# Weight sums of the first four FFN tiles: formed beside the last head's scan instead of in the FFN

## The chip, the cores and the metric

One core of a Trainium2 chip runs one layer of a diffusion backbone in float32. The metric is device time in microseconds, the median of several runs. The engines are TensorE (PE; PEld is its weight load), VectorE (DVE), ScalarE (ACT), GpSimd (POOL) and SyncE (SP), whose queue issues nearly all DMA transfers, in order.

## The reference, cut to what matters

```python
yx, _, _ = token_mixers(hx, rows, s_f, s_b, *mix_params)   # delta-rule heads | pooling, then @ w_out
x = x + gt1 * rms_norm(yx, g_post_mix)
hx = rms_norm(x, g_pre_ffn) * (1 + sc2) + sh2
x = x + gt2 * rms_norm(conv_glu_ffn(hx, w_up, conv_ffn, w_down), g_post_ffn)

def conv_glu_ffn(h, w_up, conv_w, w_down):
    gate, up = jnp.split(h @ w_up, 2, axis=-1)
    return (jax.nn.silu(depthwise_conv(gate, conv_w)) * up) @ w_down
```

There are 1024 tokens, a width of 1024, four delta-rule heads of 128, four pooling groups, and an FFN width of 2816 = 22 tiles of 128. The change touches `h @ w_up` alone: how its weights reach the matrix products.

## The kernel before, in words

**Precision.** Every float32 product is done as three products of split operands: ScalarE casts an operand to a short-mantissa high part (`split_steps`, line 259), VectorE subtracts it to get the low part. So each operand costs one ScalarE cast (`wqh`) and one VectorE subtraction (`wql`).

**Order of the work.** The kernel is a set of generators ("streams"). While the program is built, a planner (`Streams`, with the cost model `Clock`) repeatedly picks the ready stream of the lowest priority number and lets it emit its next instructions; a stream waits by yielding an event name (`signal` fires it), a count of slots (`free` returns them) or tiles that its next step reads. The outcome is a fixed instruction order on every engine and on SP's DMA queue.

**Stages around the change.** `stream_Q` (line 1098) scans the heads one after another; for head h it fires `T{h}` when it has taken three working slots, loads q, ktok and vr, forms the attention products (`dn_attn`) and then does eight scan steps (`dn_scan`, line 908), each of which goes from TensorE to VectorE (`X`), TensorE, ScalarE (`ws`, `wv`), TensorE and VectorE (`S`). Beside it `stream_G` (line 1269) runs the matrix products of the input projection as filler, with weights loaded by `stream_load`, and `pool_post` (line 1157) runs the pooling branch on VectorE. Working tiles of 128x1024 come from 13 slots (`slot`, line 282; NK = 4 and NBIG = 9). Then come the output projection in eight token tiles (`mix_load`, `stream_W`), with each tile's norm, residual and transposes (`residual`, line 1410), and the FFN.

**The up-projection.** Pairs of 512x512 blocks are multiplied by a seven-product scheme: `PROD` names, for product p = 1 to 7, its weight-side operand (block or sum of blocks of `w_up`) and its activation-side operand. Per FFN tile f the weights come as four blocks of 128x512, q11, q12, q21 and q22; four GpSimd sums form the operands of products 5, 7, 6 and 3, and products 1, 2 and 4 use q11, q12 and q22 as they are. `prep(f)` (line 1481) takes four of the eight `st` slots (NST = 8), loads the four blocks, and forms the sums in place as soon as the plain blocks have been split; since q22 is overwritten, it is loaded again for product 4 into the single buffer `st2`. Tile 2 is special: its first two operands come early as fillers and are loaded a second time into a tile `a2` of the pool `fT`. `stream_split` (line 1537) splits the operands in the order `SEQ` (line 1465) into four pairs of `wq` buffers (NWQ = 4), and `stream_up` (line 1594) does the 12 matmuls of each entry. SEQ has products 1 and 2 of tiles 0, 1 and 2 first, then the others of tiles 0 and 1, then tiles 2 to 21 interleaved by pairs. All `prep` streams start when `stream_wt` (line 1340) opens the FFN's memory at the start of the output projection. `stream_T` (line 1548) forms the activation-side sums (`T2`, `T3`, ...) and splits them.

Of the kernel before, what the change touches and what calls it, by code (L numbers as in the profile page):

```python
# [17 lines left out]
P = 128  # L18
# [7 lines left out]
NF = 22  # L26
# [101 lines left out]
class Streams:  # L128
# [10 lines left out]
    def signal(self, name):  # L139
        self.events[name] = max(self.now, self.clock.end)  # L140
# [42 lines left out]
def kernel(ctx: ExitStack, tc: tile.TileContext, I, out):  # L183
# [1156 lines left out]
    def stream_wt():  # L1340
        nonlocal wt, h2p, fa
        for e in ("Q3", "O30", "O31", "F30", "F31", "WO0", "WO1"):
            yield e
        dctx.close()
        pctx.close()
        h2p = fctx.enter_context(tc.tile_pool(name="h2", bufs=1, side="left", reuse_waits="tile"))
        for n in ("11", "21"):
            W["B" + n] = [hblock(h2p, "ha", f"b{n}{x}") for x in "hl"]
        W["hf"] = h2p.tile([P, KT, T], F32, name="hf")
        fa = fctx.enter_context(tc.tile_pool(name="ffna", bufs=1, side="left", reuse_waits="tile"))  # L1350
        wt = wctx.enter_context(tc.tile_pool(name="wtmp", bufs=2, side="left", reuse_waits="tile"))
        W["gg1"] = wt.tile([P, D], F32, name="gg1", bufs=1)
        dma(out=W["gg1"], in_=ggd[0].rearrange("k p -> (k p)").partition_broadcast(P))
        signal("WT")
        for f in range(NF):
            spawn(prep(f), 9)
        spawn(stream_split(), 8)
        spawn(stream_T(), 2)
        spawn(stream_up(), 8)
        for n, t in enumerate(ORDER):  # L1360
            if n > 1:
                yield f"H{ORDER[n - 2]}"
            W["x", t] = wt.tile([P, D], F32, name="xr")
            dma(out=W["x", t], in_=xsrc[t])
# [107 lines left out]
    CH = [f // 2 + NJ * (f % 2) for f in range(NF)]  # L1472
    A, wq, up, bank = {}, {}, {}, {}
    gd = dram.tile([NF, P, T], F32, name="gd")
    sd = dram.tile([NJ, P, 4, 512], F32, name="sd")
    td = dram.tile([NJ, P, 4, 512], F32, name="td")

    def st(name):
        return fa.tile([P, 4, P], F32, name=name, tag="st", bufs=NST)

    def prep(f):

        if f:
            yield f"pre{f - 1}"
        if f == 2:
            yield "FT"
            w = fT.tile([P, 4, 512], F32, name="a2", tag="ht", bufs=10)
            for n in range(2):
                A[f, n + 1] = w[:, n].rearrange("p (k n) -> p k n", n=P)
                dma(out=A[f, n + 1], in_=I["w_up_t"][CH[f]][:, 4 * n:4 * n + 4])  # L1490
            signal("a2")
            yield (w,)
            signal("A21")
            signal("A22")
        yield "st", 4
        src = {"11": I["w_up_t"][CH[f]][:, 0:4], "12": I["w_up_t"][CH[f]][:, 4:8],
               "21": I["w_up_t"][NF + CH[f]][:, 0:4], "22": I["w_up_t"][NF + CH[f]][:, 4:8]}
        q = {}
        for n in ("11", "21", "22", "12"):
            q[n] = st("a" + n)  # L1500
            dma(out=q[n], in_=src[n])
        signal(f"pre{f}")
        if f != 2:
            A[f, 1], A[f, 2] = q["11"], q["12"]
        yield (q["11"],)
        if f != 2:
            signal(f"A{f}1")
        yield (q["21"], q["22"])
        G.tensor_tensor(q["22"], q["21"], q["22"], ALU.add)
        A[f, 5] = q["22"]  # L1510
        yield
        G.tensor_tensor(q["21"], q["11"], q["21"], ALU.subtract)
        A[f, 7] = q["21"]
        yield f"w{f}1"
        G.tensor_tensor(q["11"], q["22"], q["11"], ALU.subtract)
        A[f, 6] = q["11"]
        yield
        signal(f"A{f}6")
        signal(f"A{f}7")
        signal(f"A{f}5")  # L1520
        yield (q["12"],)
        if f != 2:
            signal(f"A{f}2")
        yield f"w{f}2"
        G.tensor_tensor(q["12"], q["12"], q["11"], ALU.subtract)
        A[f, 3] = q["12"]
        yield
        signal(f"A{f}3")
        yield f"w{f}6"
        free("st", 1)  # L1530
        yield "st2", 1
        A[f, 4] = fa.tile([P, 4, P], F32, name="st2")
        dma(out=A[f, 4], in_=src["22"])
        yield (A[f, 4],)
        signal(f"A{f}4")

    def stream_split():
        for f, p in SEQ:
            yield "wq", 1
            yield f"A{f}{p}"  # L1540
            hi, lo = [fa.tile([P, 4, P], F32R, name=f"wq{x}", tag=f"wq{x}", bufs=NWQ) for x in "hl"]
            yield from split_steps(hi, lo, A[f, p])
            wq[f, p] = hi, lo
            signal(f"w{f}{p}")
            if p in (7, 5, 4, 3):
                free("st2" if p == 4 else "st", 1)

    def stream_T():

        nonlocal fT, fb  # L1550
        yield f"Y{ORDER[-1]}"
        hctx.close()
        fT = fctx.enter_context(tc.tile_pool(name="ffnt", bufs=1, side="right", reuse_waits="tile"))
        signal("FT")
        hf = W["hf"]
        ks = (slice(0, 2), slice(2, 4))
        b11, b12 = [hf[:, 0:4, h] for h in half]
        b21, b22 = [hf[:, 4:8, h] for h in half]
        for t in (1, 0, 2, 3):
            yield f"H{t}"  # L1560
            yield f"H{t + 4}"
            ts = slice(t * P, t * P + P)
            for x, y, z in ((b11, b12, b11), (b12, b22, b12)):
                (V if t == 3 and x is b11 else G).tensor_tensor(x[:, :, ts], y[:, :, ts], z[:, :, ts], ALU.subtract)
            yield
        wctx.close()
        yield "a2"
        fb = fctx.enter_context(tc.tile_pool(name="ffnb", bufs=1, side="left", reuse_waits="tile"))
        signal("FB")
        t2 = fT.tile([P, 4, 512], F32, name="t2f", tag="ht", bufs=10)  # L1570

        def parts(n, x, k):
            if n not in W:
                W[n] = [hblock(fT, "ht", f"{n}{y}") for y in "hl"]
            yield from split_steps(W[n][0][:, k], W[n][1][:, k], x[:, k])
            signal(f"{n}{k.start // 2}")

        for k in ks:
            V.tensor_tensor(t2[:, k], b22[:, k], b11[:, k], ALU.subtract)
        for k in ks:  # L1580
            yield from parts("T2", t2, k)
        for k in ks:
            yield from parts("T3", b12, k)
        for k in ks:
            V.tensor_tensor(b21[:, k], b21[:, k], t2[:, k], ALU.subtract)
        yield
        for n, x in (("T1", b11), ("T4", b21), ("B22", b22)):
            for k in ks:
                yield from parts(n, x, k)
        signal("TD")  # L1590
# [274 lines left out]
    spawn(stream_G(), 9)  # L1865
    spawn(stream_wt(), 2)
    spawn(stream_W(), 7)
    free("st", NST)
    free("st2", 1)
    free("wq", NWQ)  # L1870
# [77 lines left out]
```

## Time and profile before

| | us |
|---|---|
| median of three runs | 1364.37 |
| lowest, highest run | 1360.97, 1365.2 |
| the profiled execution, its own time | 1366.2 |
| its span, first to last instruction | 1364.5 |

The rows of the trace come from the profiled execution, with times in us from the span's start. A line of a timeline has start, duration, engine, line, operation, out<-in with shapes, and in brackets the idle time of the engine before it with what ended that. All instructions are recorded by one helper, line 123, so tiles tell them apart. Matmuls are pipelined, so their durations overlap.

### The profile page before, as it was taken

The numbers are of one execution on the slowest core, as the hardware profiler recorded it, in microseconds if no ns is written. First come the engines' busy times: TensorE is split into PE (matmuls) and PEld (weight loads), VectorE is DVE, ScalarE is ACT, GpSimd is POOL, SyncE is SP. The second block draws the span as 40 slices with busy tenths as digits, with TensorE's granted clock in tenths as the row PEclk, the third lists the DMA queues.
The fourth block names the chain that finished last, engine by engine and source line by source line (L and its number), as shares of the span: only waits on it lengthen the run. The fifth ranks groups of instructions, "written<-read, shape, count | busy, mean of one in ns | idle before, by whom it ended". The sixth has DMA issues, their size and how long they took to land.

```text
span 1364.5 us, 23950 instructions
## 1 busy us (share of the span) xinstructions
PE 1276.8 (94%) x8655; PEld 1006.3 (74%) x8655; DVE 1008.1 (74%) x2027; ACT 624.9 (46%) x1478; POOL 338.3 (25%) x431
## 2 busy tenths in 40 slices
PE   5878999998999799987988999999999999999997
PEld 1447668776878678856776788888888887888885
DVE  1876655656778788449879999999877778755674
ACT  3545956355676435344544333323323335644540
POOL 0562334141141510003012333333332320000122
PEclk8989989998999899988998999999999999999999
DMA  9513655545462323384322566666334339976661
GB/s 335 204 40 99 199 175 142 167 123 173 143 185 78 73 86 96 116 263 152 124 86 83 198 247 220 238 234 227 141 116 139 118 138 294 302 230 192 191 211 62
DMA packets 145302, 226.55 MB, mean 166 GB/s; under 512 B 53440, under 2 KB 66592, under 8 KB 142368
## 3 DMA queue, kind: packets, MB, share of 16 engines
q1 hardware_dynamic: 144752, 224.61, 49.9%
q8 instruction: 68, 1.11, 0.3%
q14 instruction: 50, 0.41, 0.1%
q10 hardware_dynamic: 432, 0.42, 0.1%
HBM read 164.77 MB, written 60.21 MB: 165 GB/s over the span
## 4 chain that ended last, share of the span: by engine, by line
PE 72%; DVE 13%; DMA 6%; ACT 3%; issue 3%; POOL 2%; SPq 0%; DVEq 0%; ACTq 0%; POOLq 0%
PE pa L123 27%; PE pc L123 23%; PE pb L123 22%; DVE hf L123 2%; DMA w_m<-in_wmod 1%; DMA w_mod<-in_wmod 1%; DVE x L123 1%; DVE gtmp L123 1%; POOL sX L123 1%; DVE rs_a L123 1%; POOL stmp L123 1%; DVE wql L123 1%; DVE yrs L123 1%; DMA wo_st<-in_w_out 1%; DMA sc<-blk_x 1%
## 5 line engine op out<-in xcount | busy, mean ns | idle before, releaser
L123 POOL TENSOR_TENSOR a<-a,a 128x512 f32<-128x512 f32 x88 | 143.4, 1630 | 320.4 <-DVE wql L123 158.5
L123 ACT CAST wqh<-a 128x512 fp32r<-128x512 f32 x132 | 80.9, 621 | 168.6 <-PE pb L123 76.8
L123 DVE TENSOR_TENSOR op<-dst,op 128x512 fp32r<-128x512 f32 x154 | 104.0, 715 | 58.6 <-ACT op L123 58.0
L123 PE MATMUL pa<-h_hi,w_hi 128*128 128x512 f32 x320 | 138.9, 434 | 2.5 <-ACT jk L123 1.2
L123 ACT CAST op<-dst 128x512 fp32r<-128x512 f32 x154 | 90.2, 620 | 98.6 <-PE pc L123 35.7
L123 PE MATMUL pa<-h_hi,w_lo 128*128 128x512 f32 x320 | 129.4, 404 | 1.6 <-DVE w_lo L123 1.6
L123 PE MATMUL pa<-h_lo,w_hi 128*128 128x512 f32 x320 | 130.4, 407 | 0.0
L123 PE MATMUL pc<-op 128*128 128x512 f32 x528 | 121.7, 391 | 0.0
L123 DVE TENSOR_TENSOR wql<-a,wqh 128x512 fp32r<-128x512 f32 x132 | 104.6, 795 | 17.2 <-ACT wqh L123 17.1
L123 PEld LDWEIGHTS pc<-op 128*128 128x128 f32 x528 | 99.0, 188 | 21.9 <-DVE graw L123 0.4
L123 DVE TENSOR_TENSOR hf<-hf 128x512 f32<-128x512 f32 (+1 forms) x109 | 92.3, 853 | 7.1 <-ACT hf L123 6.7
L123 POOL TENSOR_TENSOR hf<-hf,gg 128x512 f32<-128x512 f32 x16 | 21.2, 1350 | 214.2 <-ACT t L123 214.2
L123 PEld LDWEIGHTS pa<-h_hi,w_hi 128*128 128x128 f32 x320 | 61.2, 191 | 16.0 <-issue 3.0
L123 DVE SCALAR_TENSOR_TENSOR hf<-graw,sm,hf 128x1024 f32<-128x1024 f32 x44 | 71.3, 1621 | 0.7
L123 PEld LDWEIGHTS pa<-h_hi,w_lo 128*128 128x128 f32 x320 | 60.9, 190 | 14.1 <-DVE w_lo L123 1.8
L123 DVE SCALAR_TENSOR_TENSOR cv<-raw,sm,cv 128x1024 f32<-128x1024 f32 x48 | 62.6, 1305 | 11.4 <-ACT cv L123 10.8
L123 PEld LDWEIGHTS pa<-h_lo,w_hi 128*128 128x128 f32 x320 | 61.5, 192 | 9.4 <-issue 2.0
L123 PE MATMUL pa<-op 128*128 128x512 f32 x198 | 50.6, 391 | 0.0
L123 PE MATMUL pb<-op 128*128 128x512 f32 x198 | 50.4, 390 | 0.0
L123 ACT ACTIVATE hf<-hf 128x1024 f32<-128x1024 f32 x22 | 23.4, 1062 | 58.0 <-DVE hf L123 58.0
L123 ACT ACTIVATE ws<-pc,btg 128x128 f32<-128x128 f32 x80 | 27.0, 367 | 48.4 <-PE pc L123 48.0
L123 DVE TENSOR_TENSOR w_lo<-w_st,w_hi 128x512 fp32r<-128x512 f32 x40 | 27.6, 693 | 26.8 <-ACT w_hi L123 16.5
(385 smaller groups left out, 3356.4 us busy)
## 6 DMA issues: line engine op xcount, KB each, us to landing
a<-in_w_up_t SPq DMA_DIRECT2D x90, 256.0 KB, 3.2
w_m<-in_wmod SPq DMA_DIRECT2D x64, 256.0 KB, 3.3
hf<-in_w_down SPq DMA_DIRECT2D x22, 512.0 KB, 4.2
td<-hf SPq DMA_DIRECT2D x11, 1024.0 KB, 4.8
gd<-hf SPq DMA_DIRECT2D x22, 512.0 KB, 2.6
sd<-hf SPq DMA_DIRECT2D x11, 1024.0 KB, 5.4
dst<-sd SPq DMA_DIRECT2D x44, 256.0 KB, 4.5
dst<-td SPq DMA_DIRECT2D x44, 256.0 KB, 4.4
```

Source lines behind the costliest of these rows:

```text
L123: return f(*a, **k)
```

## The change

A new stream `sums_first`, with priority 6, starts at the event `T3`. For each of the tiles 0 to 3 it takes two working slots, loads the 128x1024 weights of both halves (512 KB each), forms the same four sums in place on GpSimd, and stores both to a new DRAM tensor `ad`. When all are done it fires `pre`. `prep_first` takes the place of `prep(0)` to `prep(3)`: it loads the 28 operands of these tiles one by one in the order of SEQ, each into one `st` slot, plain blocks from `w_up` and sums from `ad`. `stream_split` returns one slot for each entry of these tiles. The reload through `st2` and the tile `a2` go for tiles 0 to 3; from tile 4 on `prep` is as before, after the last of the 28 loads. Of the last four SEQ entries of tile 3, three lie behind the first entry of tile 4.

```diff
@@ -1352,7 +1352,8 @@
         W["gg1"] = wt.tile([P, D], F32, name="gg1", bufs=1)
         dma(out=W["gg1"], in_=ggd[0].rearrange("k p -> (k p)").partition_broadcast(P))
         signal("WT")
-        for f in range(NF):
+        spawn(prep_first(), 9)
+        for f in range(NPRE, NF):
             spawn(prep(f), 9)
         spawn(stream_split(), 8)
         spawn(stream_T(), 2)
@@ -1472,26 +1473,56 @@
     CH = [f // 2 + NJ * (f % 2) for f in range(NF)]
     A, wq, up, bank = {}, {}, {}, {}
     gd = dram.tile([NF, P, T], F32, name="gd")
+    NPRE = 4
+    ad = dram.tile([NPRE, 2, P, T], F32, name="ad")
     sd = dram.tile([NJ, P, 4, 512], F32, name="sd")
     td = dram.tile([NJ, P, 4, 512], F32, name="td")
 
     def st(name):
         return fa.tile([P, 4, P], F32, name=name, tag="st", bufs=NST)
 
+    def sums_first():
+
+        yield "T3"
+        for f in range(NPRE):
+            yield "s", 2
+            x = [slot("pre") for _ in range(2)]
+            for n in range(2):
+                dma(out=x[n], in_=I["w_up_t"][n * NF + CH[f]].rearrange("p k n -> p (k n)"))
+            yield tuple(x)
+            (q11, q12), (q21, q22) = [[y[:, h] for h in half] for y in x]
+            for o, y, z, op in ((q22, q21, q22, ALU.add), (q21, q11, q21, ALU.subtract), (q11, q22, q11, ALU.subtract),
+                                (q12, q12, q11, ALU.subtract)):
+                G.tensor_tensor(o, y, z, op)
+                yield
+            for n in range(2):
+                dma(out=ad[f, n], in_=x[n])
+            free_slots(*x)
+        signal("pre")
+
+    def prep_first():
+
+        yield "pre"
+        for f, p in SEQ:
+            if f < NPRE:
+                yield "st", 1
+                A[f, p] = st("ap")
+                if p in (1, 2, 4):
+                    src = I["w_up_t"][CH[f] + (NF if p == 4 else 0)][:, 0 if p == 1 else 4:4 if p == 1 else 8]
+                else:
+                    n, h = {6: (0, 0), 3: (0, 1), 7: (1, 0), 5: (1, 1)}[p]
+                    src = ad[f, n][:, half[h]].rearrange("p (k n) -> p k n", n=P)
+                dma(out=A[f, p], in_=src)
+                spawn(arrived(f, p), 9)
+        signal(f"pre{NPRE - 1}")
+
+    def arrived(f, p):
+        yield (A[f, p],)
+        signal(f"A{f}{p}")
+
     def prep(f):
 
-        if f:
-            yield f"pre{f - 1}"
-        if f == 2:
-            yield "FT"
-            w = fT.tile([P, 4, 512], F32, name="a2", tag="ht", bufs=10)
-            for n in range(2):
-                A[f, n + 1] = w[:, n].rearrange("p (k n) -> p k n", n=P)
-                dma(out=A[f, n + 1], in_=I["w_up_t"][CH[f]][:, 4 * n:4 * n + 4])
-            signal("a2")
-            yield (w,)
-            signal("A21")
-            signal("A22")
+        yield f"pre{f - 1}"
         yield "st", 4
         src = {"11": I["w_up_t"][CH[f]][:, 0:4], "12": I["w_up_t"][CH[f]][:, 4:8],
                "21": I["w_up_t"][NF + CH[f]][:, 0:4], "22": I["w_up_t"][NF + CH[f]][:, 4:8]}
@@ -1500,11 +1531,9 @@
             q[n] = st("a" + n)
             dma(out=q[n], in_=src[n])
         signal(f"pre{f}")
-        if f != 2:
-            A[f, 1], A[f, 2] = q["11"], q["12"]
+        A[f, 1], A[f, 2] = q["11"], q["12"]
         yield (q["11"],)
-        if f != 2:
-            signal(f"A{f}1")
+        signal(f"A{f}1")
         yield (q["21"], q["22"])
         G.tensor_tensor(q["22"], q["21"], q["22"], ALU.add)
         A[f, 5] = q["22"]
@@ -1519,8 +1548,7 @@
         signal(f"A{f}7")
         signal(f"A{f}5")
         yield (q["12"],)
-        if f != 2:
-            signal(f"A{f}2")
+        signal(f"A{f}2")
         yield f"w{f}2"
         G.tensor_tensor(q["12"], q["12"], q["11"], ALU.subtract)
         A[f, 3] = q["12"]
@@ -1542,8 +1570,8 @@
             yield from split_steps(hi, lo, A[f, p])
             wq[f, p] = hi, lo
             signal(f"w{f}{p}")
-            if p in (7, 5, 4, 3):
-                free("st2" if p == 4 else "st", 1)
+            if f < NPRE or p in (7, 5, 4, 3):
+                free("st2" if p == 4 and f >= NPRE else "st", 1)
 
     def stream_T():
 
@@ -1564,7 +1592,6 @@
                 (V if t == 3 and x is b11 else G).tensor_tensor(x[:, :, ts], y[:, :, ts], z[:, :, ts], ALU.subtract)
             yield
         wctx.close()
-        yield "a2"
         fb = fctx.enter_context(tc.tile_pool(name="ffnb", bufs=1, side="left", reuse_waits="tile"))
         signal("FB")
         t2 = fT.tile([P, 4, 512], F32, name="t2f", tag="ht", bufs=10)
@@ -1865,6 +1892,7 @@
     spawn(stream_G(), 9)
     spawn(stream_wt(), 2)
     spawn(stream_W(), 7)
+    spawn(sums_first(), 6)
     free("st", NST)
     free("st2", 1)
     free("wq", NWQ)
```

## Rows read from the trace of the kernel before

**Rows 1.** The page, part 1: busy us (share of the span) and instructions by engine.

```profile
PE 1276.8 (94%) x8655; PEld 1006.3 (74%) x8655; DVE 1008.1 (74%) x2027; ACT 624.9 (46%) x1478; POOL 338.3 (25%) x431
```

**Rows 2.** Table by stage: stretch, length, engines' busy us (count), clock, DMA share, GB/s.

```profile
900.00:1000.00 100.00, 100.00 (x433) 80.95 (x432) 88.32 (x104) 31.76 (x51) 36.05 (x32) 1.00 0.50 180
```

**Rows 3.** TensorE's timeline, 619 to 642 us: start, us, operation, [idle before <-releaser].

```profile
621.38 0.50 PE L123 MATMUL pc<-wo_h,mxl 128*128 128x512 f32 x1 [2.33 <-DVE mxl L123]
...
631.28 1.97 PE L123 MATMUL pb<-cst,xr 128*128 128x128 f32 x8 [4.63 <-DVE xr L123]
...
633.48 0.63 PE L123 MATMUL pc<-wo_h,mxh 128*128 128x512 f32 x1
...
636.47 0.63 PE L123 MATMUL pc<-wo_h,mxl 128*128 128x512 f32 x1
...
638.17 0.39 PE L123 MATMUL pc<-wo_h,mxl 128*128 128x512 f32 x1
```

**Rows 4.** Table by stage, the 10 us behind TensorE's long wait (columns as in rows 2).

```profile
630.00:640.00 10.00, 8.71 (x31) 7.34 (x32) 7.90 (x20) 4.69 (x9) 0.00 (x0) 0.66 0.44 152
```

**Rows 5.** GpSimd's timeline, 605 to 640 us: first and last of three bursts (eight adds).

```profile
614.16 4.03 POOL L123 TENSOR_TENSOR a<-a,a 128x512 f32<-128x512 f32 x3 [73.01 <-DVE rs_h L123]
...
624.92 4.47 POOL L123 TENSOR_TENSOR a<-a,a 128x512 f32<-128x512 f32 x3 [2.45 <-DVE wql L123]
```

**Rows 6.** VectorE's timeline, 612 to 638 us; the last three start after GpSimd is done.

```profile
614.38 1.08 DVE L123 SCALAR_TENSOR_TENSOR yrs<-rs_a,yrs 128x1 f32<-128x1 f32 x1
...
617.17 1.04 DVE L123 SCALAR_TENSOR_TENSOR yrs<-rs_a,yrs 128x1 f32<-128x1 f32 x1
...
619.58 1.75 DVE L123 TENSOR_TENSOR mxl<-mx,mxh 128x512 fp32r<-128x512 f32 x1
621.25 2.30 DVE L123 TENSOR_TENSOR x<-x,xr 128x1024 f32<-128x1024 f32 x1
...
625.34 1.71 DVE L123 TENSOR_TENSOR wql<-a,wqh 128x512 fp32r<-128x512 f32 x1
...
631.45 0.16 DVE L123 SCALAR_TENSOR_TENSOR yrs<-rs_a,yrs 128x1 f32<-128x1 f32 x1
...
635.41 1.22 DVE L123 TENSOR_TENSOR x<-x,xr 128x1024 f32<-128x1024 f32 x1
...
637.14 0.69 DVE L123 TENSOR_TENSOR mxl<-mx,mxh 128x512 fp32r<-128x512 f32 x1
```

**Rows 7.** Waits of TensorE, 735 to 765 us: us in total, times, longest.

```profile
PE pb L123 <- ACT wqh L123: 0.8, 1, 0.8
PE pb L123 <- DVE wql L123: 0.6, 1, 0.6
PE pb L123 <- DVE graw L123: 0.4, 1, 0.4
```

**Rows 8.** VectorE's timeline, 724 to 742 us: two pairs of the same shape.

```profile
724.69 3.44 DVE L123 TENSOR_TENSOR T3l<-hf,T3h 128x1024 fp32r<-128x1024 f32 x2
...
739.17 2.35 DVE L123 TENSOR_TENSOR T4l<-hf,T4h 128x1024 fp32r<-128x1024 f32 x2
```

**Rows 9.** Waits of ScalarE, 765 to 1100 us: the longest group.

```profile
ACT wqh L123 <- PE pb L123: 100.0, 49, 2.2
```

**Rows 10.** SyncE's timeline: the first load of the last head's scan.

```profile
476.01 0.34 SPq L123 DMA_DIRECT2D q<-qkvd  x1
```

**Rows 11.** The page, part 5: the GpSimd adds of the weight sums, all 22 tiles.

```profile
L123 POOL TENSOR_TENSOR a<-a,a 128x512 f32<-128x512 f32 x88 | 143.4, 1630 | 320.4 <-DVE wql L123 158.5
```

**Rows 12.** Table by stage: head 2's scan, and the stretch from 480 us on.

```profile
450.00:470.00 20.00, 16.42 (x98) 14.10 (x96) 16.30 (x39) 10.72 (x35) 15.23 (x33) 0.91 0.18 44
480.00:530.00 50.00, 50.00 (x658) 40.72 (x658) 44.76 (x121) 23.24 (x66) 3.54 (x15) 1.00 0.31 98
```

**Rows 13.** Waits of TensorE, 450 to 470 us.

```profile
PE pc L123 <- DVE S L123: 1.8, 3, 0.8
PE pc L123 <- DVE X L123: 0.6, 1, 0.6
```

## The prediction

> **What bounds the kernel now.** I read the page's busy line first: TensorE is busy for 1276.8 of 1364.5 us [rows 1], so time can only come out of its idle stretches or out of stretches at the lower clock. The table by stage then shows where these are not: 900 to 1000 us has 432 or so matmuls without a gap at full clock [rows 2], and the stages of the FFN from about 765 us on look the same. Whatever the change shifts there is worth nothing, and whatever is won ahead of it carries through to the end. The timeline of TensorE gives the gaps ahead of 765 us. At the start of the output projection it waits 2.33 us for `mxl` and 4.63 us for `xr`, both made by VectorE, and after the second wait the granted clock of the stretch is 0.66: eight of its matmuls run at the lower of the two levels (1.2 GHz), 0.63 us each where they take 0.39 us a little later [rows 3, 4].
>
> The reader should now lay two timelines of that stretch beside each other. GpSimd works on the weight sums of FFN tiles 0 and 1 in three bursts, eight adds of 128x512 [rows 5]. VectorE, in just these microseconds, has operations that take far longer than the same operation a little later: `yrs` 1.08 against 0.16, `mxl` 1.75 against 0.69, the 1024-wide `x` add 2.30 against 1.22, `wql` 1.71 against 0.69 for the same shape [rows 6]. Each ends about when a GpSimd add ends. All of these read two operands from SBUF; so do the adds. This hold of one engine by the other is what the change moves.
>
> **The change, part by part.**
>
> *Taken away at the start of the output projection.* The eight adds of tiles 0 and 1 no longer run there. VectorE gets back three `yrs` (0.92, 0.88 and one between: 2.7 us), one `mxl` (1.06), one `x` (1.08) and one `wql` (1.02): 5.8 us, or 0.73 us for each of the eight adds [rows 5, 6]. The first 3.7 us of this come ahead of the `mxl` that TensorE waits 2.33 us for, so that wait goes. Then `xr` is ready 5.8 us earlier while TensorE arrives only 2.33 us earlier, so about 4.63 - 3.5 = 1.1 us of its second wait stays. TensorE is thus 5.8 us ahead when the matmuls behind it begin. With a wait of 1.1 us in place of 4.63 I expect full clock behind it: eight matmuls at 0.63 become 0.39, 8 x 0.24 = 1.9 us [rows 3]. Together 7.7 us. Bounds: nothing, if something else is late next (the `mx` loads, which share SP's queue with the operand loads); 2.33 + 4.63 + 1.9 = 8.9 us if all of it goes. I take the 7.7, near the upper end, because the stretched operations are the ones in the chain itself.
>
> *The operand loads.* Eight slots are filled in the order of use, as eight were before; as the first four splits free theirs, four more loads of 256 KB come, each behind a split in SP's in-order queue and ahead of later `mx` loads. Before, these slots stayed full until the up-projection. A split is one cast and one `wql` of 0.69 us [rows 6]; I put the wait of SP at no more than 2 us and, since `mx` is itself released by VectorE, at nothing in the sum. What covers it is the lead of one `mx` tile; without that it costs those 2 us.
>
> *Taken away at the start of the up-projection.* The sums of tiles 2 and 3 and the one-buffer reload of the fourth operand (`st2`) go from 725 to 763 us. TensorE's waits there are 0.8, 0.6 and 0.4 us: for the cast of the reloaded operand, for a `wql`, for an eviction on VectorE [rows 7]. VectorE's pair `T3l` takes 3.44 us under the adds, the like pair `T4l` without them 2.35 [rows 8], so about 1.1 us for such a pair. I take 1.7 of the 1.8 us of waits. Bounds: 0 to 1.8. The gap ahead of `T2` lies behind VectorE's residual chain and stays.
>
> *Tile 4, the first that is prepared the old way.* It needs four slots at once, and with all 28 loads of tiles 0 to 3 queued one by one ahead of it, it gets them after the split of (2,3), two entries ahead of its own first entry, where before it was four or five ahead. ScalarE's casts in this stretch wait for TensorE, 100.0 us in 49 waits [rows 9]: splits run the full four `wq` buffers ahead, that is 4 x 12 matmuls. Cost 0, at most one entry (12 x 0.23 us, from 432 in 100 us [rows 2]: 2.8 us) if that lead is not there yet.
>
> *Added in the last head's scan.* The event `T3` comes with the load of `q` at 476.0 us [rows 10]. From there sixteen adds at a mean of 1.63 us [rows 11] are 26 us of GpSimd, and with a load and a store of 1 MB ahead of and behind each four, they stretch over some 45 us, from about 482 to 527. No wait of TensorE is covered there: it is busy for 50.00 of the 50 us from 480 to 530, with matrix products as filler, and VectorE for 44.76 [rows 12]. The scan's steps cross from TensorE to VectorE and back every few microseconds, and the instructions of both are in a fixed order, so a held VectorE operation becomes a wait of TensorE once the 5.24 us of VectorE's idle time are used up. At 0.73 us for each add, 16 x 0.73 = 11.7 us of hold, less 5.24: 6.4 us. A second estimate from 450 to 470 us, where head 2's scan ran beside 15.23 us of GpSimd work: TensorE waited 1.8 + 0.6 = 2.4 us for `S` and `X` [rows 12, 13]; scaled by 26/15.23 that is 4.1 us. I take 5.5, nearer the first because those instructions are short and the adds are long. Bounds: 0, and 18.6 (below). The 8 loads and 8 stores of 512 KB meet a DMA share of 0.31 [rows 12]; the stores wait in SP's queue for the last add, with the `w_st`, `inv` and `odram` transfers behind them. `w_st` has a lead of about a job of 48 matmuls, so this costs nothing unless SP stands for over 10 us.
>
> The sum: 5.5 - 7.7 - 1.7 = -3.9 us. The profiled execution took 1366.2 us, so it would be 1362.3; it stands 1.8 us above the median of 1364.37, against which I forecast 1360.5. A measurement of this kernel can tell some 0.3%, 4.1 us, from no change, so the forecast lies on that edge.
>
> **The rivals.**
>
> A, *the scan hides it all*: VectorE's held work is mostly the pooling branch, which is not needed at once. Then -9.4 us: 1355.0. For it: the scan has a chain of its own beside the filler, and VectorE some idle time. Against: in-order queues put `X` and `S` behind the held operation. Chance 0.18. Here belongs also the case that the change does not do what it says, because the two slots come free only after head 3 and the sums run at 560 to 600 us beside an idle GpSimd: the same time. At `T3` eight of thirteen slots are taken and the pooling branch has one, so I give that 0.03 of it.
>
> B, *slower*: each add holds VectorE for its whole length. The place is 482 to 527 us, the price 16 x 1.49 us (4.47 us for three adds [rows 5]) = 23.8, less 5.24: 18.6, net +9.2: 1373.6. It decides from a mean hold of (9.4 + 5.24 + 4.1)/16 = 1.17 us per add. Against it: the eight adds seen cost 0.73. For it: VectorE is fuller here, so more adds meet an operation with two SBUF inputs. Chance 0.20, with the lower end at that point.
> The Trainium skill, page "SBUF — State Buffer", section "Who interferes with whom", says that a VectorE instruction with two SBUF inputs and a GpSimd instruction that reads SBUF exclude each other, and that the one that issues second blocks fully until the first is done. By that rule alone the price is B's; the trace agrees on the kind of operation (`yrs` at 1.08 us), and its 0.73 us says that an operation mostly arrives when part of the add is over.
>
> C, *the output projection stays bound by loads*: only the 2.33 us wait goes. Then 5.5 - 2.3 - 1.7 = +1.5: 1365.9. For it: the operand loads freed by the splits are new in SP's queue there. Chance 0.17.
>
> **How the numbers follow.** The forecast has 0.45; with its terms uncertain by some 4 us about half of it is beyond -4.1. Faster: 0.18 + 0.27 = 0.45. Same: 0.18 + 0.14 = 0.32. Slower: 0.20 + 0.03 = 0.23. The range runs from 1351 (A with all 8.9 us of the projection and 2 us more) to 1372, within B; it leaves out its upper half, about 0.1, and as much of chance below. Forecast's own range: 1356 to 1365.
>
> **What would show it.** Right: sixteen GpSimd adds between 480 and 530 us, waits of TensorE for `X`, `S` or VectorE's copies there that sum to 4 to 7 us; no add from the scan's end until tile 4's; `yrs` at 0.16 us throughout; the waits for `mxl` and `xr` under 1.5 us in sum and no stretch at 0.66 behind them; the waits for `wqh` and `wql` at 743 us gone. Wrong: waits of TensorE in the scan under 2 us or over 10, a wait for an `mx` load in place of `xr`, or a gap at tile 4.

## The result and the profile after

The changed kernel takes 1377.1 us (median of six runs, 1375.0 to 1384.9) against 1364.4 for the kernel before beside it: ratio 1.0094, 95% interval 1.0071 to 1.0118. It is slower by 12.8 us (0.0094 x 1364.4); the forecast was 1360.5 and its range ended at 1372. Below, times "against before" are always worked out so, from a run's ratio, since the median of before moves by a microsecond or two from one set of runs to the next. By the 95% intervals each such number is good to 2 to 4.5 us, and a difference of two of them to some 3 to 5 us.

Where it went is read first from four marks on the time axis: the load of `q` [rows 10], the start of the last matmul of the input projection (operands `h_hi` and `h_lo`; below, the last `pa<-h`), the first of W_out (`wo_h`), the first of the up-projection (`b11h`). They divide the spans of the two profiled executions (1364.5 and 1374.0 us) so:

| us | before | changed | difference |
|---|---|---|---|
| start to `q` | 476.0 | 472.7 | -3.3 |
| scan and projection: `q` to last `pa<-h` | 105.8 | 119.2 | +13.4 |
| handover: to first `wo_h` | 5.7 | 21.3 | +15.6 |
| W_out: to first `b11h` | 113.6 | 101.7 | -12.0 |
| the rest | 663.4 | 659.2 | -4.2 |

The gain is there, in the last two lines, though a part of the -12.0 belongs to W_out's late start (see e2). The scan cost more than twice what was forecast, and the handover, which no step of the prediction dealt with, is the largest loss.

The page's busy line and its group of FFN sums, which answer to [rows 1] and [rows 11] (72 additions in the FFN where there were 88):

```profile
PE 1274.0 (93%) x8655; PEld 1005.6 (73%) x8655; DVE 1001.4 (73%) x2027; ACT 623.8 (45%) x1478; POOL 336.9 (25%) x431
...
L123 POOL TENSOR_TENSOR a<-a,a 128x512 f32<-128x512 f32 x72 | 118.9, 1652 | 216.1 <-DVE wql L123 133.5
```

**The scan.** The table by stage, changed kernel, the stretch of [rows 12]:

```profile
480.00:530.00 50.00, 42.61 (x525) 33.72 (x524) 42.38 (x79) 17.41 (x48) 27.31 (x26) 0.93 0.55 192
```

TensorE was busy for all 50.00 us of it; now 7.4 us are missing. VectorE's 42.38 us look like the 44.76 of before, but it got through 79 instructions in place of 121: a held instruction, one that ends late because an addition is running, counts as busy. Its timeline shows them, held ones among free ones of like shape:

```profile
487.60 1.22 DVE L123 SCALAR_TENSOR_TENSOR ors<-rs_a,ors 128x4 f32<-128x4 f32 x1
...
496.97 1.70 DVE L123 TENSOR_TENSOR w_lo<-w_st,w_hi 128x512 fp32r<-128x512 f32 x1
...
508.69 0.69 DVE L123 TENSOR_TENSOR inv<-cbuf,inv 128x512 f32<-128x512 f32 x1
...
518.22 1.23 DVE L123 TENSOR_TENSOR inv<-cbuf,inv 128x512 f32<-128x512 f32 x1
...
530.36 0.68 DVE L123 TENSOR_TENSOR w_lo<-w_st,w_hi 128x512 fp32r<-128x512 f32 x1
```

Summed over the scan (each operation against the median of the same operation and shape in kernels without the additions), the excess is some 10.3 us, 0.65 for each of the 16 additions; nearly all of it sits in 13 held operations. TensorE's longest waits from 478 to 560 us, of 9.0 us in all, where the kernel before had none:

```profile
PE pc L123 <- DVE S L123: 3.8, 2, 2.2
PE pb L123 <- DVE W L123: 2.1, 1, 2.1
PE pb L123 <- DVE E L123: 1.3, 1, 1.3
PE pb L123 <- ACT N L123: 1.0, 1, 1.0
```

**The handover.** TensorE's timeline after its last input-projection matmul, at 591.85:

```profile
600.21 0.80 PE L123 MATMUL pa<-pmh,pwh 128*128 128x512 f32 x1 [7.97 <-ACT pmh L123]
603.91 0.79 PE L123 MATMUL pa<-pml,pwh 128*128 128x512 f32 x1 [2.91 <-DVE pml L123]
...
613.11 0.80 PE L123 MATMUL pa<-wo_h,mxh 128*128 128x512 f32 x1 [5.58 <-ACT mxh L123]
```

It waits for the last pooling group (`pmh`, `pml`), then for the first tile of the mix, whose load can only follow that group's store of the first half of the tokens. The same two places in the kernel before, where the last `pa<-h` starts at 581.82:

```profile
583.39 0.51 PE L123 MATMUL pa<-pmh,pwh 128*128 128x512 f32 x1 [1.18 <-ACT pmh L123]
...
587.49 1.22 PE L123 MATMUL pa<-wo_h,mxh 128*128 128x512 f32 x2 [2.53 <-ACT mxh L123]
```

SP's queue, before and then changed:

```profile
576.44 0.37 SPq L123 DMA_DIRECT2D mixd<-raw  x1
...
582.57 0.33 SPq L123 DMA_DIRECT2D mx<-mixd  x1
...
586.43 0.38 SPq L123 DMA_DIRECT2D mixd<-raw  x1
...
589.21 2.14 SPq L123 DMA_DIRECT2D mixd<-zo  x4
```

```profile
599.57 0.89 SPq L123 DMA_DIRECT2D mixd<-zo  x2
...
606.07 2.60 SPq L123 DMA_DIRECT2D mixd<-raw  x2
609.50 0.33 SPq L123 DMA_DIRECT2D mx<-mixd  x1
```

Before, the last two pooling stores stood among those of the output gates (`mixd<-zo`), and the first load of the mix went out between the two; now both stand behind all of the gates. GpSimd's timeline offers a ready cause, and it was my first theory: the small memsets that border the pooling buffers stand in its in-order queue behind additions that wait for loads (columns end in the idle time ahead and what ended it).

```profile
496.85 8.68 POOL L123 TENSOR_TENSOR pre<-pre 128x512 f32<-128x512 f32 x5 [3.35 <-DMA pre<-in_w_up_t]
508.26 0.21 POOL L123 MEMSET rbuf<- 128x64 f32 x2 [2.73 <-DMA ad<-pre]
512.21 6.69 POOL L123 TENSOR_TENSOR pre<-pre 128x512 f32<-128x512 f32 x4 [3.75 <-DMA pre<-in_w_up_t]
...
525.72 4.33 POOL L123 TENSOR_TENSOR pre<-pre 128x512 f32<-128x512 f32 x3 [6.03 <-DMA pre<-in_w_up_t]
533.10 0.21 POOL L123 MEMSET rbuf<- 128x64 f32 x2 [3.05 <-DMA ad<-pre]
```

**W_out.** What [rows 3, 4, 6] showed stretched is at its short length, and behind its first 12 us, which have a granted clock of 0.82, the stage runs at full clock (VectorE's timeline, then a row of the table by stage):

```profile
641.66 0.69 DVE L123 TENSOR_TENSOR mxl<-mx,mxh 128x512 fp32r<-128x512 f32 x1
...
643.38 0.14 DVE L123 SCALAR_TENSOR_TENSOR yrs<-rs_a,yrs 128x1 f32<-128x1 f32 x1
```

```profile
640.00:650.00 10.00, 10.00 (x48) 8.24 (x47) 8.07 (x25) 5.58 (x13) 0.00 (x0) 1.00 0.37 135
```

### The profile page after: what moved, and what is told of

Read it like the earlier page. It is cut to its first block, busy times and chain, and to the rows that moved or that the text cites. A ratio compares the mean times of both kernels' runs of the same rounds, so it can differ in the third digit from the quotient of the medians.

```text
span 1374.0 us, 24008 instructions
## 1 busy us (share of the span) xinstructions
PE 1274.0 (93%) x8655; PEld 1005.6 (73%) x8655; DVE 1001.4 (73%) x2027; ACT 623.8 (45%) x1478; POOL 336.9 (25%) x431
## 4 chain that ended last, share of the span: by engine, by line
PE 71%; DVE 13%; DMA 6%; issue 3%; POOL 3%; ACT 3%; SPq 1%; DVEq 0%; ACTq 0%; POOLq 0%
PE pa L123 24%; PE pc L123 24%; PE pb L123 22%; POOL sX L123 2%; POOL stmp L123 1%; DVE rs_a L123 1%; DMA w_mod<-in_wmod 1%; DVE hf L123 1%; DVE x L123 1%; DVE gtmp L123 1%; DMA sB<-blk_i 1%; DMA mx<-mixd 1%; SPq L123 1%; DMA sc<-blk_x 1%; DVE cv L123 1%
## 5 line engine op out<-in xcount | busy, mean ns | idle before, releaser
L123 POOL TENSOR_TENSOR a<-a,a 128x512 f32<-128x512 f32 x72 | 118.9, 1652 | 216.1 <-DVE wql L123 133.5
L123 ACT CAST wqh<-a 128x512 fp32r<-128x512 f32 x108 | 65.8, 621 | 147.6 <-PE pb L123 56.3
L123 DVE TENSOR_TENSOR wql<-a,wqh 128x512 fp32r<-128x512 f32 x108 | 82.6, 768 | 20.7 <-ACT wqh L123 20.7
L123 DVE SCALAR_TENSOR_TENSOR hf<-graw,sm,hf 128x1024 f32<-128x1024 f32 x44 | 67.8, 1540 | 0.7
L123 POOL TENSOR_TENSOR hf<-hf 128x512 f32<-128x512 f32 x7 | 10.5, 1501 | 162.0 <-DVE yrs L123 149.5
```

The costliest lines, as they stand in the source:

```text
L123: return f(*a, **k)
```

## The experiments

In the order in which they ran. **First the two sides alone, and the two suspects on the cost side.**

**e1, the gain alone.**

```diff
-    spawn(sums_first(), 6)
+    signal("pre")
-                    src = ad[f, n][:, half[h]].rearrange("p (k n) -> p k n", n=P)
+                    src = I["w_up_t"][n * NF + CH[f]][:, 4 * h:4 * h + 4]
```

> The gain side alone: no sums are formed during the scan, and the first four tiles' sum operands are loaded one by one from the plain weights, the same bytes (the sums of these four tiles are left out of the computation). The forecast's gain terms say -7.7 at W_out and -1.7 at the up-projection's start, so 1364.4 - 9.4 = about 1355 us. Theory A (the gain terms were right, and all of the miss is on the cost side) expects 1355, within 3. Theory B (the 11.9 us regained inside W_out in the changed kernel were in part its late start being caught up, as operands lay ready before it began) expects less: 1359 to 1364.

Measured: ratio 0.9927 (0.9912 to 0.9942), -10.0 us. Theory A. Its waits of TensorE from 586 to 700 us have 2.5 us left for `xr` (6.0 before) and 0.2 for `mxl` (2.3 + 0.2 before), and only 0.7 us for `wo_h` is new:

```profile
PE pa L123 <- ACT mxh L123: 2.7, 2, 2.1
PE pb L123 <- DVE xr L123: 2.5, 3, 1.6
...
PE pa L123 <- DVE mxl L123: 0.2, 1, 0.2
```

**e2, the cost alone**: `sums_first`, unchanged, added to the kernel before.

> The cost side alone: the kernel before, with the sums of four tiles formed and spilled during the last head's scan, and never used. The forecast's cost term was +5.5, so 1370. Theory A (scan +13 and late handover +15.6, both real costs of forming the sums there, of which W_out regains nothing here since its own GpSimd work is in place) expects 1364.4 + 13 to 1364.4 + 28, that is 1377 to 1392, with the first W_out matmul 20 us or more later than before. Theory C (the late handover came with another order of the pooling and output-gate steps, which the changed FFN also decides) expects 1375 to 1379: scan later by 10 to 13, the handover as before.

Measured: 1.0164 (1.0147 to 1.0181), +22.4 us, with a handover of 22.0 us. Theory A. And -10.0 + 22.4 = 12.4 is the change's 12.8: the sides add up. Yet W_out takes 106.7 us here against 113.6 before, with its own GpSimd additions in place: after a late handover a part of the loss comes back there.

**e3, no additions; e4, tiny ones.** The planner (`clock.note`) still counts all 16.

```diff
-                G.tensor_tensor(o, y, z, op)
+                streams.clock.note("POOL", "tensor_tensor", (o, y, z, op), {})
+                G.eng.tensor_tensor(o[:, 0:8], y[:, 0:8], z[:, 0:8], op)     # e4 only
```

> The changed kernel with the loads and stores of the sums tiles kept and the 16 additions left out (so what is stored is the plain weights, and the sums of four tiles are left out of the computation). The order given out by the planner counts them as before. Theory H1 (an addition on GpSimd holds VectorE's operations on SBUF: worth 10 us in the scan) expects the last input-projection matmul some 10 us earlier, near 582. Theory H2 (GpSimd's queue: the pooling branch's memsets stand behind additions that wait for their loads) expects the pooling branch on time and the handover, 21.3 us in the changed kernel, back near 6. Both: 1355 to 1358. H1 alone: 1377 - 10 = 1367, handover still over 15. H3 (the transfers themselves, SP's queue or the slot buffers): within 4 us of 1377.

> The changed kernel with each of the 16 additions cut to 8 columns of 512 (the rest of the sums is left out of the computation): they wait for their loads in GpSimd's queue as before, but run a small part of the time. H1 (VectorE held while an addition runs) expects the scan's 10 us back, like the kernel without additions. H2 (GpSimd's queue) expects the pooling branch's memsets still late behind the loads, so the handover from input projections to W_out still 15 us or more, and a total near 1367, some 10 above the kernel without additions. If H2 is wrong, the two kernels agree within 3 us.

Measured: e3 1.0009 (0.9997 to 1.0022), e4 1.0020 (1.0004 to 1.0036). The additions are worth (1.0094 - 1.0009) x 1364.4 = 11.6 us, and the scan of e3 is short again (108.4 us from `q` to the last `pa<-h`). But its handover is 22.3 us, with nothing on GpSimd that could stand in the way, and e4's waits in that queue add only 1.5 us. So GpSimd's queue, my first theory, is not what delays the handover.

**Then the order, and what would undo it.**

**e5, the order alone.** The loads, the additions and the stores become notes to the planner; the program has none of them. The operands are the plain weights, as in e1.

```diff
-                dma(out=x[n], in_=I["w_up_t"][...])
+                streams.clock.note("SP", "dma_start", (), dict(out=x[n], in_=I["w_up_t"][...]))
...
-                dma(out=ad[f, n], in_=x[n])
+                streams.clock.note("SP", "dma_start", (), dict(out=ad[f, n], in_=x[n]))
```

> The changed kernel with nothing of the sums emitted: no loads, no additions, no stores in the scan (the sums of four tiles are left out; their operands are the plain weights, as in the run of the gain alone). Only the planner counts the sums as if they were there, so the order given out is the changed kernel's. In the kernel without additions the time from the last input-projection matmul (581.8 us) to the first W_out matmul (603.7 us) was 21.9 us, though nothing ran on GpSimd any more. Theory P (the late handover comes from the order of the instructions: the planner, counting the sums on its DMA queue and on GpSimd, gives the two th buffers to the output gate first and to the last pooling group last) expects a handover of 18 us or more here too, and a total of 1356.2 + 11 = 1367. Theory T (the sums' transfers and slot buffers delay the pooling branch on the chip) expects a handover near 6 us and 1356, as in the run of the gain alone.

Measured: 1.0016 (1.0002 to 1.0030). Theory P. TensorE's timeline has the late handover of the changed kernel, wait for wait, in a program without one byte or addition of the sums:

```profile
589.30 0.79 PE L123 MATMUL pa<-pmh,pwh 128*128 128x512 f32 x1 [8.68 <-ACT pmh L123]
592.80 0.79 PE L123 MATMUL pa<-pml,pwh 128*128 128x512 f32 x1 [2.71 <-DVE pml L123]
...
602.21 0.79 PE L123 MATMUL pa<-wo_h,mxh 128*128 128x512 f32 x1 [5.88 <-ACT mxh L123]
```

The order costs (1.0016 - 0.9927) x 1364.4 = 12.1 us; the handover is 16.7 us longer than in e1 (22.0 against 5.3), and W_out gives 3.6 back (100.8 against 104.4). And e3, which has the transfers, is not above e5 (-1.0 us, good to 3): the 8 MB of loads and stores cost nothing that can be measured. In e3, though, no store waits for an addition.

**e6, the borders on VectorE.**

```diff
-            G.memset(buf[:, 0:left], 0.0)
+            V.memset(buf[:, 0:left], 0.0)
...
-                G.memset(buf[:, left + n:n + w - 1], 0.0)
+                V.memset(buf[:, left + n:n + w - 1], 0.0)
```

> The changed kernel with one edit: the borders of the pooling branch's row and column buffers are zeroed on VectorE instead of GpSimd, so that they stand behind no addition, in the planner's count and on the chip; the order then has both halves of the last pooling group ahead of the last two output gates again, as before the change. All sums are formed in the scan as in the change. Theory P expects the handover back at 6 to 10 us and 1377.1 - 11 = 1366, with the scan still 10 to 13 us late. If GpSimd's queue and the order had no part in it, 1377 as before.

Measured: 0.9993 (0.9974 to 1.0013), 13.8 us below the changed kernel, with a handover of 4.2 us:

```profile
596.84 0.73 PE L123 MATMUL pa<-wo_h,mxh 128*128 128x512 f32 x2 [3.14 <-ACT mxh L123]
```

**e7 and e8, the sums after the scan.** e7: one generator per tile, all waiting for `Q3`. e8: the edit of e6, and the one generator waiting for `Q3`. In both, `stream_wt` waits for `pre` too.

```diff
-        yield "T3"
+        yield "Q3"
```

> The sums moved out of the scan: the four tiles' loads start when the last head's scan has ended, all four at once in eight slots, additions and stores follow. VectorE's held operations in the scan go: last input-projection matmul back near 582. Theory P says that the order gets worse, not better, since the planner now puts the last pooling group behind these loads and additions: handover 18 us or more, total 1364 to 1368. A theory by which only the hold in the scan costs anything expects 1356 to 1359.

> Both edits: the sums formed after the scan, one tile after the other in two slots, and the borders zeroed on VectorE. The scan is free of additions, the pooling branch stands behind none of them, but the sums end some 60 us after the scan and the FFN's pools open behind them. If hold and order are the two costs and the late end of the sums costs nothing: 1356 to 1359. If W_out's stretch pays for additions that now run beside it (VectorE held for 0.65 us each, 16 of them: at most 10 us, of which W_out took 5.8 before): 1360 to 1366.

Measured: 1.0074 (1.0047 to 1.0100) and 1.0070 (1.0037 to 1.0103). Both worse than any theory said. The trace of e7 says that the edit did not do what it was meant to (the additions, with durations in ns, then first and last start in us; and SP's queue):

```profile
L123 POOL TENSOR_TENSOR pre<-pre x16: 1264/1288/1996, 494.4 to 570.4; 128x512 f32<-128x512 f32 x16
```

```profile
475.72 0.50 SPq L123 DMA_DIRECT2D pre<-in_w_up_t  x1
477.69 0.33 SPq L123 DMA_DIRECT2D q<-qkvd  x1
```

The additions begin at 494.4 us, in the scan, and in SP's queue the first load of the sums stands ahead of the load of `q`, which is emitted before the scan starts: the built program's order is not only that of the emission. e7 has hold and late handover (20.6 us) together. e8's additions are late (547.6 to 590.5), but its handover is 16.8 us; why the borders on VectorE do not help there is not shown.

**e9, the turn of the `th` buffers.** To e5: an output gate asks for its buffer after the pooling half that went ahead of it before the change.

```diff
+            if h:
+                yield ("t11", "t00", "t01")[h - 1]
             yield "th", 1
...
             yield "th", 2
+            signal(f"t{gi}{hf}")
```

> As the run of the order alone (nothing of the sums emitted, the sums of four tiles left out, the planner counting them), with one edit: the output gates of heads 1, 2 and 3 ask for their th buffers only after the pooling halves that stood ahead of them before the change. Theory P, narrowed to the turn of the two th buffers, expects the first W_out matmul within 10 us of the last input-projection matmul and a total of 1356 to 1359. If the lateness lies elsewhere in the planner's order (the pooling branch's own steps are put later, whoever gets the buffers), the handover stays over 15 us and the total near 1367.

Measured: 0.9961 (0.9942 to 0.9979), handover 15.1 us. Between the two: 7.5 of the 12.1 us are the turn of these buffers; the rest I put down to the pooling steps themselves, which the planner still emits later; no run shows that by itself.

**e10, no additions (e3) and the borders on VectorE (e6); e11, those borders in the kernel before.**

> Both costs taken away: the additions left out (loads and stores of the sums tiles kept; the sums of four tiles are left out of the computation) and the borders of the pooling buffers zeroed on VectorE. If the hold in the scan (10 us: 1377.1 to 1367.3) and the order at the handover (11 us: 1377.1 to 1365.7) are two separate costs that add up, 1377.1 - 10 - 11 = 1356, the run of the gain alone; the transfers then cost nothing. If they overlap, or if the transfers cost something of their own, 1360 to 1366.

> A control: the kernel before, with the borders of the pooling buffers zeroed on VectorE and nothing else. Theory P says that the edit helps the changed kernel only by undoing the order that the sums brought, so here it is worth nothing: 1364 to 1368. If the edit is a gain by itself of 5 us or more (below 1361), the changed kernel with this edit tells less about the order.

Measured: e10 0.9942 (0.9919 to 0.9966), 2 us from e1, so hold and order are separate and nearly add up. e11 1.0018 (0.9991 to 1.0045): the edit of e6 is no gain by itself. In that order, though, the additions cost (0.9993 - 0.9942) x 1364.4 = 7.0 us, not 11.6 (each good to some 4), and the excess of VectorE's operations beside them, counted as above, is 8.0 us, not 10.3. The short handover of e6 has to be read with its total: with these borders on VectorE the input projection itself ends later, 114.2 us after `q` in e10 against 108.4 in e3.

**e12, two tiles after the scan**: `if f == 2: yield "Q3"` in the loop of `sums_first`, borders of pooling groups 0 and 1 on VectorE.

> A candidate: two tiles' sums in the scan, the other two after its end, and the borders of the last two pooling groups (those behind additions) zeroed on VectorE. Eight additions in the scan hold VectorE for half of what 16 did (5 us in place of 10), and the order has the last pooling half just before the loads of the mix. By the two costs: 1356.2 + 5 = 1361, faster than both kernels. If the other eight additions, now beside the output gates and the pooling branch, cost the same 0.65 us each on the path, 1366; if the handover is late again, 1372.

Measured: 1.0033 (1.0009 to 1.0056), handover 12.7 us. A miss, like e8: the pooling branch was late again.

**Last, the order of before with real sums**, which the planner is not told of (`nc.gpsimd`, `nc.sync` in place of `G`, `dma`).

**e13, in the scan**: a tile's additions after every second step.

> The sums of all four tiles formed in the scan as in the change, but the planner does not count them, so the order of everything else is that of the run of the gain alone; a tile's additions are given out with every second step of the scan. If order (12.2 us) and hold (11.6 us) are two costs and the order's is the planner's alone, the handover is under 10 us and the total is 1364.4 - 10 + 11.6 = 1366, at most 3 less if the additions fall where VectorE is idle. If the pooling branch's memsets behind the additions in GpSimd's queue delay it on the chip too, the handover grows to 15 us or more and the total to 1372 or more.

Measured: 1.0022 (1.0003 to 1.0041), handover 6.2 us, scan 119.3 us. So the additions, with their loads and stores, cost (1.0022 - 0.9927) x 1364.4 = 13.0 us, 11.2 of them between `q` and the last `pa<-h` (e1: 108.1); the excess of VectorE's operations is 12.2 us. With the order of before the handover is on time though every addition, load and store is there, and the working slots are taken as in the change; so neither GpSimd's queue nor the slots make it late.

**e14 and e15, after the scan.** A copy of one column ties each load to the scan's last output; the additions are emitted after the last pooling border (`rb0`), and `stream_wt` waits for `pre`, as in e7.

```diff
+                nc.vector.tensor_copy(x[n][:, 0:1], src[:, 0:1])
+                nc.sync.dma_start(out=x[n], in_=I["w_up_t"][...])
...
+                nc.gpsimd.dma_start(out=ad[f, n], in_=x[n])     # e14; e15: nc.sync
```

> A candidate that takes both costs away: the order of before (the planner does not count the sums), the eight loads tied to the last step of the scan by a copy of one column into each tile, the additions after the pooling branch's last memset on GpSimd, the stores issued by GpSimd itself. VectorE is busy 5.0 of 20 us in 560:580 in the kernel before, so additions there should hold little. By the two costs: 1356 to 1360, faster than both kernels. If the additions reach into 580:640, where W_out needs VectorE, or their 4 MB of loads and 4 MB of stores delay the loads of W_out and of the mix: 1362 to 1368.

> The same, with the stores in SP's queue, where all eight stand ahead of the loads and stores of the output gates of heads 2 and 3 and of W_out's last loads. If a store that waits for its additions holds up what is queued behind it, the handover is later than in the run with stores on GpSimd by the wait of the last addition, some 5 to 15 us, and the total 3 to 10 us above it. If SP's queue has slack there, the two agree within 3 us.

Measured: e14 0.9973 (0.9953 to 0.9993), -3.7 us, short of what was expected. It is the one kernel with the whole computation whose interval lies below 1, but the medians of the two sets agree (1365.4 and 1365.3), so a gain over before is hardly shown; over the changed kernel it is 16.5 us. e15 1.0004 (0.9986 to 1.0021), with a handover of 13.4 us against 6.1: the issue of its eight stores takes SP's queue from 574.87 to 583.63 us, ahead of a pooling store and of gate loads. In the total e15 stands 4.2 us above e14, at the edge of what these runs can tell apart. VectorE's timeline of e14 shows what is left:

```profile
551.45 0.16 DVE L123 TENSOR_TENSOR rs_a<-rs_a,ors 128x4 f32<-128x4 f32 x1
...
552.71 1.25 DVE L123 SCALAR_TENSOR_TENSOR ors<-rs_a,ors 128x4 f32<-128x4 f32 x1
553.89 0.68 DVE L123 TENSOR_TENSOR inv<-cbuf,inv 128x512 f32<-128x512 f32 x1
554.49 1.25 DVE L123 TENSOR_TENSOR rs_a<-rs_h,ors 128x4 f32<-128x4 f32 x1
...
558.01 2.74 DVE L123 SCALAR_TENSOR_TENSOR ors<-rs_a,ors 128x4 f32<-128x4 f32 x1
...
562.60 0.16 DVE L123 SCALAR_TENSOR_TENSOR ors<-rs_a,ors 128x4 f32<-128x4 f32 x1
```

The operation of 2.74 us ends with the second of these two additions on GpSimd:

```profile
558.24 2.49 POOL L1506 TENSOR_TENSOR pre<-pre 128x512 f32<-128x512 f32 x2
```

The last head's output norm, operations on 128x4 that take 0.16 us when free, needs 11 us for eight of them, and TensorE waits for it:

```profile
563.25 0.77 PE L123 MATMUL pb<-cst,o 128*128 128x128 f32 x2 [6.47 <-ACT o L123]
```

**e16, as e14, the loads tied to the last output tile after that norm.**

> As the candidate with GpSimd's stores, with the loads tied to the last head's last output tile instead of the last step of the scan, so that no addition runs beside the output norm's chain. If the hold of that chain (6.5 us of TensorE's wait) is what was left of the cost, the total is 5 to 6 us below that candidate: 1364.4 x 0.9973 - 6 = 1355 to 1358, ratio about 0.993, the run of the gain alone. If the additions, now some 10 us later (562 to 588), hold the output gates' multiplies and the splits of W_out instead, it stays at 1360 to 1363.

Measured: 1.0030 (1.0010 to 1.0051), above both expectations. VectorE's and TensorE's timelines:

```profile
568.43 10.80 DVE L123 TENSOR_TENSOR zo<-zt,zo 128x256 f32<-128x256 f32 x4 [10.27 <-DMA zo<-odram]
...
589.48 1.43 DVE L123 TENSOR_TENSOR zo<-zt,zo 128x256 f32<-128x256 f32 x4 [2.04 <-DMA zo<-odram]
```

```profile
580.51 0.80 PE L123 MATMUL pa<-pmh,pwh 128*128 128x512 f32 x1 [10.38 <-ACT pmh L123]
```

The norm is free, but the next chain is held instead: four gate multiplies take 10.80 us beside the additions and 1.43 without. VectorE stood idle for 10.27 us just ahead of them; that it has idle time says nothing about whether a hold costs.

## Why the prediction was wrong

The sum of the runs, each step one part of the change against before (the steps good to 2 to 4 us):

| | ratio | us | the step adds |
|---|---|---|---|
| the operand loads, no sums (e1) | 0.9927 | -10.0 | -10.0 |
| and the planner's order (e5) | 1.0016 | +2.2 | +12.1 |
| and the transfers (e3) | 1.0009 | +1.2 | -1.0 |
| and the additions: the change | 1.0094 | +12.8 | +11.6 |

**The gain was right in the main**: -9.4 forecast, -10.0 measured. W_out was to give 7.7 and gave 9.2 (e1: 104.4 us from the first `wo_h` to the first `b11h`, 113.6 before), mostly by the waits that were named (`xr` and `mxl`, 5.8 us less); the up-projection's start 1.7, and 2.7 came behind that mark (660.7 against 663.4). That the sum came so close is partly luck: both parts went beyond their upper bounds (8.9 and 1.8), and e1's profiled execution has a scan 2.3 us longer than before. At the up-projection's start the three waits of [rows 7] are gone, but the gap ahead of `T2`, which was to stay, grew from 3.0 to 4.8 us (waits of TensorE, before from 701 to 801 us, then e1 from 694 to 793, the longer of two):

```profile
PE pb L123 <- DVE T2l L123: 1.6, 1, 1.6
```

```profile
PE pb L123 <- ACT T2h L123: 2.7, 1, 2.7
```

So TensorE's waits behind the mark are only 0.8 us shorter in sum (6.4 against 7.2). Where the rest of the 2.7 us comes from is not shown; the granted clock of the 100 us behind the mark is 0.97 in e1 and 0.95 before.

Tile 4 at nothing held: in the changed kernel TensorE has no wait from 748 to 800 us. The operand loads in SP's queue at nothing held too, and rival C with it falls.

**The scan was mis-sized**, +5.5 for 11.6 (13.0 in e13). The hold itself was right: 0.73 us an addition, 11.7 in all, against 0.65 and 10.3 in the trace. The step that failed is "less 5.24": it took VectorE's idle time [rows 12] as slack that the hold would use up first. The runs show none of that: in each of three orders the loss is as large as the whole hold, to within the noise: 11.6 for a hold of 10.3 in the change (against e3), 13.0 for 12.2 in e13 (against e1), 7.0 for 8.0 in e6 (against e10); the last, good to some 4 us, would by itself fit the 6.4 of the first estimate too. These losses include what the stores' waiting for additions costs: in the changed kernel SP stands 15.9 us for them in six waits, the longest 6.4, but none of TensorE's waits in the scan is for a tile that SP loads. The likely reason, argued and not tried, is that this idle time lies in the chain's own waits, on either side of each step, so that a longer step lengthens the chain and leaves the idle time as it was. The second estimate, scaled from head 2's scan (4.1), was lower still and is refuted by the same numbers. Rival A falls; its case of late slots too, since the first addition ran at 485 us. Rival B came nearest in time (1373.6) for the wrong reason: its price of a whole addition each, 18.6 us, was not paid. In the scan the 13 held operations lost 0.8 us each in the mean, less than the 1.26 of a whole addition, so most came when one was partly over. For the Trainium skill's rule (page "SBUF — State Buffer", section "Who interferes with whom") that the engine which issues second blocks until the first is done, the trace agrees in e14 where an operation of 0.16 us takes 1.25, and differs where one takes 2.74 and outlasts two additions.

**The handover was missed**, 0 for 12.1. The step is the sentence on the 8 loads and 8 stores, which "costs nothing unless SP stands for over 10 us". On the chip they cost nothing that can be measured (e3 against e5). But this kernel's order comes from a planner that counts them, and the additions, on its own clocks; counted, they make the pooling steps and their requests for the two `th` buffers late, so that the output gates went first: the late handover is there when they are counted and not emitted (e5, 22.0 us), and gone when they are emitted and not counted (e13, 6.2 us). The prediction priced each instruction that is added and never asked what the added ones do to the order of those that stay. The list of what would show it wrong had no gap between the input projection and W_out either.

## What to carry to other kernels

Where a program's order is planned from costs, an addition of work has two prices: what it does on the chip, and what its counted cost does to everybody else's order; a build in which the work is counted but not emitted, beside one in which it is emitted but not counted, separates them. Idle time of an engine is not by itself slack for a hold: beside this scan it took up none of it in three orders, so the safer forecast adds the hold in full, unless the held operations are known to be off the chain. And a move of work out of one stage is judged by both stages alone, gain without cost and cost without gain, before anything is made of the sum.

## What was not expected of the hardware

One GpSimd addition of 128x512 took 1.26 us at the least, yet a single VectorE operation of 128x4 was held for 2.74 us (e14), and four of 128x256 for 9.4 us together beside eleven microseconds of additions (e16): a held operation lost its turn to more than one addition. And 8 MB of extra loads and stores in the scan, at a DMA share of 0.71 in e3's 480 to 530 us, against 0.30 in e5's, made no difference that can be measured (-1.0 us, good to 3; tables by stage, e3 and then e5, the DMA share next to last):

```profile
480.00:530.00 50.00, 49.15 (x585) 40.08 (x584) 41.07 (x108) 22.66 (x65) 3.71 (x13) 0.98 0.71 239
```

```profile
480.00:530.00 50.00, 48.94 (x591) 39.85 (x590) 44.07 (x115) 23.62 (x67) 3.12 (x12) 1.00 0.30 85
```
